# A gate's arithmetic behind the copies of all its banks, and kept-weight casts tied to the products

## The chip, the cores and the metric

The kernel runs on one core of one Trainium2 chip. The metric is device time: the microseconds (us) from start to end of one execution. The engines are named as in the profile: PE is TensorE (PEld its weight loads), DVE is VectorE, ACT is ScalarE, POOL is GpSimd, SP is SyncE, which here only issues DMAs.

## The reference, cut to what matters

One step of a hybrid decoder layer: eight heads of stick-breaking attention and four heads of gated linear attention (GLA) read one common input projection; each head's output is gated and goes through one output projection, with a norm and a residual behind it.

```python
u = h @ w_in                                   # h: rms_norm(x); sq, sk, sv, sg | gq, gk, gv, gg, ga
o_sb  = sb_prompt(q, k, v, sb_bias)            # 8 heads, 1040 positions (16 meta + 1024)
o_gla = rms_norm(gla_prompt(gq, gk, gv, gf), gla_norm_g)
mixed = concatenate([o_sb * silu(sg), o_gla * silu(gg)])
x = x + rms_norm(mixed @ w_out, norm_post_g)   # w_out: 2048 x 2048
```

The same is done for 8 sampled sequences of 4 tokens with a paged key and value cache. The change touches two pieces: `o * silu(g)` for the gates `sg` and `gg`, and the weights of the last product of `mixed @ w_out`.

## The kernel before, in words

*Input projection and gates.* `inproj` (L336) computes 128 columns of `w_in` for all tokens: 16 blocks of depth, three matmuls for each (high and low halves of both factors), the tokens in three chunks, each in a PSUM bank of its own (`acc_..._0` to `_2`; the pool has three such banks). Weights come in four chunks `wr`, are cast to `wh` on ScalarE (L187), and their rest `wl` is made on VectorE (L190). A chunk of weights thus serves four blocks of depth. When a bank is complete, `evac` is called. For a gate, `gate_group` (L528), it copies the bank to a stage `gx` on ScalarE (L532), after which the bank is free for the next group, and hands `gate_rest` (L507) to the weaver. That loads the head's output `go` from the DRAM tensor `od` (L513), and makes silu as a clamp (L516, VectorE), Exp and Ln (L517, L518, ScalarE), a maximum (L519, VectorE), Exp (L520, ScalarE), two products (L521 with `gx`, L522 with `go`, VectorE), and stores the result to `md` (L523). There are 16 gates, so 48 such pieces. `gx`, `go` and `gs` take buffers of one pool, `stg`, that has seven; a gate takes nine.

*The weaver.* `W.spawn(gen, d)` puts a piece of work on a heap; `W.beat()`, called after each two blocks of depth of a chunk, runs what is due. A gate's rest is spawned with a delay of 1, so it is written at the beat right behind its own bank's copy. The queues' order is then set by the framework's scheduler from the order of writing, from priorities (`urgent()` raises weight casts and bank copies) and from dependences; a NOSYNC dependence (`tc.add_manual_dep`) only says that one instruction stands behind another and puts no wait into the program. Each engine runs its own queue in order.

*Around gates 0 to 2.* Gate 0 runs beside the tail of the last attention head (`z`, `X`, `Y`, `hi_s`, `lo_s`, L596 to L663). VectorE meanwhile works through L470, the products of sampled queries with cached keys (`z_feed`). `od<-ost` (L687) stores the last head's output; `wal` (L861) is a cast that waits for it, for the tile that it writes lies in memory that the store reads from. After gate 2 comes the group `acc_gk` of the GLA keys.

*Output projection.* Seven products of halves (a Strassen-like scheme) for each half `q` of the columns: `step(p, q)` takes eight weight blocks `wr` from a ring of four (cast L1480 on ScalarE, rest L1481 on VectorE), and accumulates into four banks `b`, twelve matmuls for each block (L1682 to L1684). Products 7 and 4 share banks: after product 7 `take` reads them (L1547, `y`), then product 4 adds to the same banks, after which `take` reads them again (L1551, `u`). Sixteen small matmuls `sc` (L1702) for the sampled tokens end a product 7. The very last product, 4 of the second half, takes its weights from `kept`, loaded ahead by `load_keep` (L1713): eight loads `keep`, eight casts (L1723, ScalarE), eight subtractions (L1724, VectorE). `spread(ins)` (L480) puts an instruction behind `W.mark`, the newest product matmul, order only.

Of the kernel before, what the change touches and what calls it, by code (L numbers as in the profile page):

```python
# [10 lines left out]
F32 = mybir.dt.float32  # L11
# [4 lines left out]
AF = mybir.ActivationFunctionType  # L16
# [38 lines left out]
NOSYNC = mybir.DependencyInfo(mybir.DependencyClass.NoSync, mybir.DependencyReason.DATA)  # L55
# [34 lines left out]
def hybrid_step(ctx: ExitStack, tc: tile.TileContext, x_prompt, x_sample, cache_k, cache_v, state_gla,  # L90
# [5 lines left out]
    vec, act, pool = nc.vector, nc.scalar, nc.gpsimd  # L96
# [17 lines left out]
    W = Weaver()  # L114

    def stage(nm, dt=F32):
        return stg.tile([P, 384], dt, tag="stg", name=nm)
# [77 lines left out]
    with tc.tile_pool(name="xp", bufs=2) as xp, tc.tile_pool(name="xps", bufs=5, space=PSUM) as xps:  # L195
# [109 lines left out]
        for c, (lo, hi) in enumerate(XCHUNKS):  # L305
            n = hi - lo
            for k in range(NK):
# [10 lines left out]
                ins = act.activation(hh[k][:, lo:hi], ps[:, :n], AF.Copy, scale=gpre[:, k:k + 1]).ins  # L318
# [11 lines left out]
            for k in range(NK):  # L330
                wh, wl = wchunks[k]
# [4 lines left out]
    def inproj(c0, evac, lo0, nm, chunks=CHUNKS):  # L336

        acc = [accp.tile([P, 512], F32, tag="acc", name=f"acc_{nm}_{c}") for c in range(3)]
        for kk in range(NK // 2):
            if kk % 2 == 0:  # L340
                ws = weight_chunk(w_in[0], kk // 2, c0, f"{nm}_{kk // 2}")
            for c, (lo, hi) in enumerate(chunks):
                lo = max(lo, lo0)
                n = hi - lo
                for k in (2 * kk, 2 * kk + 1):
                    wh, wl = ws[k % 4]
                    mm(acc[c][:, :n], wh, hh[k][:, lo:hi], start=(k == 0), stop=False)  # L347
                    mm(acc[c][:, :n], wh, hl[k][:, lo:hi], start=False, stop=False)  # L348
                    W.mark = mm(acc[c][:, :n], wl, hh[k][:, lo:hi], start=False, stop=(k == NK - 1)).ins  # L349
                if kk == NK // 2 - 1:  # L350
                    with urgent():
                        evac(c, acc[c][:, :n], lo, hi)
                W.beat()
# [126 lines left out]
    def spread(ins):  # L480

        if W.mark is not None:
            tc.add_manual_dep(ins.ins, W.mark.name, NOSYNC, reason="spread")
# [24 lines left out]
    def gate_rest(g, lo, hi, x):  # L508
        n = hi - lo
        e = min(hi, REAL) - lo  # L510
        o = stage(f"go{g}_{lo}")
        w = n if g >= 8 else e
        nc.sync.dma_start(o[:, :w], od[g][:, lo - META:lo - META + w])  # L513
        st = stage(f"gs{g}_{lo}")
        s, x = st[:, :n], x[:, :n]
        vec.tensor_scalar(s, x, -1.0, 30.0, ALU.mult, ALU.min)  # L516
        act.activation(s, s, AF.Exp)  # L517
        act.activation(s, s, AF.Ln, bias=1.0)  # L518
        vec.scalar_tensor_tensor(s, x, -1.0, s, ALU.mult, ALU.max)  # L519
        act.activation(s, s, AF.Exp, scale=-1.0)  # L520
        vec.tensor_tensor(s, s, x, ALU.mult)  # L521
        vec.tensor_tensor(s[:, :w], s[:, :w], o[:, :w], ALU.mult)  # L522
        nc.sync.dma_start(md[g][:, lo - META:hi - META], s)  # L523
        return
        yield

    evacs = []

    def gate_group(g):
        def evac(c, ps, lo, hi):  # L530
            x = stage(f"gx{g}_{c}")
            evacs.append(act.copy(x[:, :hi - lo], ps).ins)  # L532
            W.spawn(gate_rest(g, lo, hi, x), 1)
        inproj(C_SG + g * P if g < 8 else C_GG + (g - 8) * P, evac, META, f"g{g}")


# [260 lines left out]
    with tc.tile_pool(name="gp", bufs=1) as gp, tc.tile_pool(name="gps", bufs=1, space=PSUM) as gps:  # L797
# [20 lines left out]
        def slot(c):  # L818

            return 8 if c == 8 else 4 * (1 - c % 2) + c // 2  # L820
# [540 lines left out]
    with ExitStack() as out:  # L1361
# [99 lines left out]
        def behind_ring(ins):  # L1461
            tc.add_manual_dep(ins, newest[0].name, NOSYNC, reason="behind")
# [251 lines left out]
        def load_keep():  # L1714

            keep.extend(slot(REGION["B"][i], f"keep{i}") for i in range(4))
            kept.extend([keep[k // 2][:, (2 * (k % 2) + i) * 512:(2 * (k % 2) + i + 1) * 512] for i in range(2)] for k in range(8))
            for k in range(12):
                if k < 8:
                    behind_ring(nc.sync.dma_start(kept[k][1].bitcast(F32), td[3][:, k, 512:1024]).ins)  # L1720
                if k > 3:
                    wh, wl = kept[k - 4]
                    act.copy(wh, wl.bitcast(F32))  # L1723
                    vec.tensor_tensor(wl, wl.bitcast(F32), wh.bitcast(F32), ALU.subtract)  # L1724
                yield 2

        kept = []
        AFTER = {(1, 1): lambda: W.spawn(form(5, 2)), (2, 1): lambda: W.spawn(form(3, 2), 8), (6, 1): lambda: W.spawn(form(7, 2)),
                 (5, 1): lambda: W.spawn(form(4, 1)),
                 (3, 1): lambda: (W.spawn(finish0()), W.spawn(load_keep(), 1))}  # L1730
        for pair in ((1, 2), (6,), (5, 3), (7, 4)):
            for q in range(2):
# [48 lines left out]
```

## Time and profile before

| | us |
|---|---|
| median of three runs | 2034.35 (2033.86 to 2036.96) |
| the profiled execution's own time | 2034.71 |
| its span, first to last instruction | 2033.0 |
| PE busy | 2004.2 (99%) |
| DVE busy | 1496.9 (74%) |
| ACT busy | 1018.4 (50%) |

Engine times are sums over the span. A matmul's duration in the trace is longer than the distance to the next one's start, since matmuls overlap; what a matmul costs is read from the distance of starts. A bracket behind an instruction gives the idle time of its engine ahead of it and what ended that time.

### The profile page before, as it was taken

The page shows a single profiled execution, that of the slowest core. Times are in us where ns is not written, and L with a number is a line of the kernel's source. Part 1 is how long each engine was busy: PE and PEld are TensorE (multiplying, and loading weights), DVE is VectorE, ACT ScalarE, POOL GpSimd, SP SyncE. Part 2 cuts the span into 40 slices and gives each one's busy share as a digit, 9 for nine tenths or more (in the row PEclk, how much of TensorE's full clock was granted, in tenths as well). Part 3 has the DMA queues.
Part 4 walks back from the last instruction along what each step waited for, and adds up shares of the span by engine and source line. Part 5 has one row for each costly group of instructions (what it writes and reads, how often), then busy time and mean ns, then how long its engine had stood idle before and what let it go on. Part 6 is the DMA issues. An engine that isn't in the chain of part 4 may idle for free.

```text
span 2033.0 us, 41746 instructions
## 1 busy us (share of the span) xinstructions
PE 2004.2 (99%) x12379; PEld 1852.4 (91%) x12379; DVE 1496.9 (74%) x6163; ACT 1018.4 (50%) x2377; POOL 96.1 (5%) x355
## 2 busy tenths in 40 slices
PE   6999999999999999999999999999999999999998
PEld 5999999999999999999999999999988898788776
DVE  7368888888888888899898888978444338365466
ACT  7356767675766757433535335254433335343342
POOL 0111110101000010000000000000000000000000
PEclk9999999999999999999999999999999999999999
DMA  6345554545555442433342434335767656352485
GB/s 205 98 136 161 143 163 132 175 129 157 151 161 151 141 125 77 142 101 89 103 108 80 126 79 120 90 93 176 243 220 234 221 186 221 104 176 94 141 281 204
DMA packets 371980, 301.92 MB, mean 149 GB/s; under 512 B 42336, under 2 KB 312264, under 8 KB 371752
## 3 DMA queue, kind: packets, MB, share of 16 engines
q1 hardware_dynamic: 371448, 298.73, 49.1%
q8 instruction: 97, 1.59, 0.3%
q14 instruction: 131, 1.07, 0.2%
q10 hardware_dynamic: 304, 0.53, 0.1%
HBM read 241.84 MB, written 57.31 MB: 147 GB/s over the span
## 4 chain that ended last, share of the span: by engine, by line
PE 91%; DVE 3%; DMA 2%; ACT 2%; issue 1%; SPq 0%; DVEq 0%; POOL 0%; POOLq 0%; ACTq 0%
PE acc_g L347 6%; PE acc_g L348 5%; PE acc_g L349 5%; PE b L1682 4%; PE b L1683 4%; PE b L1684 4%; PE acc_gv L347 3%; PE acc_gv L348 3%; PE acc_gv L349 3%; PE acc_k L347 3%; PE acc_k L349 3%; PE acc_k L348 3%; PE acc_q L348 3%; PE acc_q L347 3%; PE acc_q L349 3%; PE acc_v L347 3%
## 5 line engine op out<-in xcount | busy, mean ns | idle before, releaser
L470 DVE SCALAR_TENSOR_TENSOR jk<-kp,qb 128x128 f32<-128x128 f32 x2048 | 593.6, 290 | 46.2 <-DMA qb<-qsd 3.0
L347 PE MATMUL acc_g<-hT,wh_g 128*128 128x368 f32 (+2 forms) x768 | 250.7, 326 | 0.0
L348 PE MATMUL acc_g<-hT,wh_g 128*128 128x368 f32 (+2 forms) x768 | 247.2, 322 | 0.0
L349 PE MATMUL acc_g<-hT,wl_g 128*128 128x368 f32 (+2 forms) x768 | 246.9, 321 | 0.0
L470 DVE DVE_READ_ACCUMULATOR jk<-kp,qb 128x1 f32 x2048 | 167.3, 82 | 0.0
L1682 PE MATMUL b<-ring,f 128*128 128x512 f32 x416 | 163.9, 394 | 1.5 <-DVE y L1547 1.1
L1683 PE MATMUL b<-ring,f 128*128 128x512 f32 x416 | 162.3, 390 | 0.0
L1684 PE MATMUL b<-ring,f 128*128 128x512 f32 x416 | 161.9, 389 | 0.0
L347 PEld LDWEIGHTS acc_g<-hT,wh_g 128*128 128x128 f32 x768 | 144.3, 188 | 12.0 <-issue 10.7
L348 PEld LDWEIGHTS acc_g<-hT,wh_g 128*128 128x128 f32 x768 | 144.4, 188 | 0.7
L349 PEld LDWEIGHTS acc_g<-hT,wl_g 128*128 128x128 f32 x768 | 144.2, 188 | 0.0
L1481 DVE TENSOR_TENSOR ring<-wr,ring 128x512 fp32r<-128x512 f32 x104 | 71.2, 689 | 97.7 <-ACT ring L1480 97.1
L1480 ACT CAST ring<-wr 128x512 fp32r<-128x512 f32 x104 | 64.0, 620 | 134.7 <-PE b L1684 78.1
L347 PE MATMUL acc_gv<-hT,wh_gv 128*128 128x402 f32 (+2 forms) x384 | 130.1, 339 | 0.0
L347 PE MATMUL acc_k<-hT,wh_k 128*128 128x384 f32 (+1 forms) x384 | 126.1, 328 | 0.0
L348 PE MATMUL acc_gv<-hT,wh_gv 128*128 128x402 f32 (+2 forms) x384 | 125.3, 326 | 0.0
L349 PE MATMUL acc_gv<-hT,wl_gv 128*128 128x402 f32 (+2 forms) x384 | 125.0, 326 | 0.0
L349 PE MATMUL acc_k<-hT,wl_k 128*128 128x384 f32 (+1 forms) x384 | 124.7, 325 | 0.0
L348 PE MATMUL acc_k<-hT,wh_k 128*128 128x384 f32 (+1 forms) x384 | 124.4, 324 | 0.0
L347 PE MATMUL acc_q<-hT,wh_q 128*128 128x368 f32 (+2 forms) x384 | 124.3, 324 | 0.0
L348 PE MATMUL acc_q<-hT,wh_q 128*128 128x368 f32 (+2 forms) x384 | 123.6, 322 | 0.0
L349 PE MATMUL acc_q<-hT,wl_q 128*128 128x368 f32 (+2 forms) x384 | 123.3, 321 | 0.0
(483 smaller groups left out, 5263.6 us busy)
## 6 DMA issues: line engine op xcount, KB each, us to landing
kp<-in_cache_k_dram SPq DMA_DIRECT2D x512, 64.0 KB
vr<-in_cache_v_dram SPq DMA_DIRECT2D x64, 512.0 KB
qb<-qsd SPq DMA_DIRECT2D x64, 256.0 KB
wr_g<-in_w_in_dram SPq DMA_DIRECT2D x64, 256.0 KB
wr<-td SPq DMA_DIRECT2D x56, 256.0 KB
tf<-in_w_out_dram SPq DMA_DIRECT2D x48, 256.0 KB
td<-tf SPq DMA_DIRECT2D x48, 256.0 KB
wr<-in_w_out_dram SPq DMA_DIRECT2D x48, 256.0 KB
```

Of the source, the lines that this page charges most:

```text
L347: mm(acc[c][:, :n], wh, hh[k][:, lo:hi], start=(k == 0), stop=False)
L348: mm(acc[c][:, :n], wh, hl[k][:, lo:hi], start=False, stop=False)
L349: W.mark = mm(acc[c][:, :n], wl, hh[k][:, lo:hi], start=False, stop=(k == NK - 1)).ins
L470: ins = vec.scalar_tensor_tensor(jk[:], kp[:], 1.0, qbs[h, b][:, t, :], ALU.mult, ALU.mult, accum_out=zt[:, t, NPG - 1 - i:NPG - i])
L1480: act.copy(wh, r)
L1481: vec.tensor_tensor(wl, r, wh.bitcast(F32), ALU.subtract)
L1682: mm(bk[:], ah, wh, start=first and k == 0, stop=False, skip_group_check=True)
L1683: mm(bk[:], ah, wl, start=False, stop=False, skip_group_check=True)
L1684: W.mark = mm(bk[:], al, wh, start=False, stop=last and k == 7, skip_group_check=True).ins
```

## The change

Two edits. In `gate_rest` the first Exp stands, by an order-only dependence, behind the newest bank copy, and the rest of bank `c` is spawned with a delay of 3 − c beats instead of 1: all three rests of a gate are now written at the same beat, behind the copy of the third bank. In `load_keep` the cast of a kept weight is put behind the newest product matmul. One line is added, so lines of the new kernel beyond 517 count one more.

```diff
--- before.py
+++ after.py
@@ -514,7 +514,8 @@
         st = stage(f"gs{g}_{lo}")
         s, x = st[:, :n], x[:, :n]
         vec.tensor_scalar(s, x, -1.0, 30.0, ALU.mult, ALU.min)
-        act.activation(s, s, AF.Exp)
+        ins = act.activation(s, s, AF.Exp)
+        tc.add_manual_dep(ins.ins, evacs[-1].name, NOSYNC, reason="behind")
         act.activation(s, s, AF.Ln, bias=1.0)
         vec.scalar_tensor_tensor(s, x, -1.0, s, ALU.mult, ALU.max)
         act.activation(s, s, AF.Exp, scale=-1.0)
@@ -530,7 +531,7 @@
         def evac(c, ps, lo, hi):
             x = stage(f"gx{g}_{c}")
             evacs.append(act.copy(x[:, :hi - lo], ps).ins)
-            W.spawn(gate_rest(g, lo, hi, x), 1)
+            W.spawn(gate_rest(g, lo, hi, x), 3 - c)
         inproj(C_SG + g * P if g < 8 else C_GG + (g - 8) * P, evac, META, f"g{g}")
 
 
@@ -1720,7 +1721,7 @@
                     behind_ring(nc.sync.dma_start(kept[k][1].bitcast(F32), td[3][:, k, 512:1024]).ins)
                 if k > 3:
                     wh, wl = kept[k - 4]
-                    act.copy(wh, wl.bitcast(F32))
+                    spread(act.copy(wh, wl.bitcast(F32)))
                     vec.tensor_tensor(wl, wl.bitcast(F32), wh.bitcast(F32), ALU.subtract)
                 yield 2
```

The number of instructions on each engine is the same. What stands where, at three places (names are tile and buffer number; an output stands ahead of `<-`):

ScalarE after gate 2; `gx` is a bank's copy, `gs_16` and `gs_384` the first and second piece of the gate's arithmetic, `wh_gk` a weight cast of the next group. Before:

```order
L532 COPY gx_0_15356<-acc_g_0_14983 128x368
L517 ACTIVATE gs_16_15360<-gs_16_15360 128x368
L532 COPY gx_1_15375<-acc_g_1_14984 128x384
L518 ACTIVATE gs_16_15360<-gs_16_15360 128x368
L532 COPY gx_2_15415<-acc_g_2_14985 128x304
L187 CAST wh_gk_1_15569<-wr_gk_1_15567 128x512
L520 ACTIVATE gs_16_15360<-gs_16_15360 128x368
L517 ACTIVATE gs_384_15400<-gs_384_15400 128x384
```

Now:

```order
L533 COPY gx_0_15356<-acc_g_0_14983 128x368
L533 COPY gx_1_15364<-acc_g_1_14984 128x384
L187 CAST wh_gk_1_15569<-wr_gk_1_15567 128x512
L533 COPY gx_2_15393<-acc_g_2_14985 128x304
L517 ACTIVATE gs_16_15397<-gs_16_15397 128x368
L519 ACTIVATE gs_16_15397<-gs_16_15397 128x368
L517 ACTIVATE gs_384_15408<-gs_384_15408 128x384
L519 ACTIVATE gs_384_15408<-gs_384_15408 128x384
```

The copies of the three banks moved ahead of all of the gate's activations.

ScalarE after gate 1, before and now; `wal` is the cast that waits for the store of `ost`, `wh_g_2` and `wh_g_3` are gate 2's third and fourth weight chunk. Before:

```order
L517 ACTIVATE gs_768_14974<-gs_768_14974 128x304
L518 ACTIVATE gs_768_14974<-gs_768_14974 128x304
L520 ACTIVATE gs_768_14974<-gs_768_14974 128x304
L187 CAST wh_g_2_15189<-wr_g_2_15187 128x512
L861 CAST wal_15489<-walr 96x128
L187 CAST wh_g_3_15290<-wr_g_3_15288 128x512
```

Now:

```order
L521 ACTIVATE gs_16_14952<-gs_16_14952 128x368
L521 ACTIVATE gs_384_14963<-gs_384_14963 128x384
L862 CAST wal_15489<-walr 96x128
L517 ACTIVATE gs_768_14974<-gs_768_14974 128x304
L187 CAST wh_g_2_15189<-wr_g_2_15187 128x512
L519 ACTIVATE gs_768_14974<-gs_768_14974 128x304
L521 ACTIVATE gs_768_14974<-gs_768_14974 128x304
L187 CAST wh_g_3_15290<-wr_g_3_15288 128x512
```

`wal` moved from behind the cast of the third weight chunk to a place ahead of it, and the third piece's activations to both sides of that cast.

VectorE at the end of product 7, first half; `y_0_0` to `y_0_3` are the reads of the four banks, `keep` a kept weight, `c` finished rows of the output. Before:

```order
L1481 TENSOR_TENSOR ring_29084<-wr_7_31006,ring_29083 128x512
L1616 SCALAR_TENSOR_TENSOR c_0_29119<-c_0_29119,vrt_y_30857,xr_0_30869 128x512
L1481 TENSOR_TENSOR ring_29084<-wr_0_31054,ring_29083 128x512
L1724 TENSOR_TENSOR keep_30878<-keep_30878 128x512
L1616 SCALAR_TENSOR_TENSOR c_1_29120<-c_1_29120,vrt_y_30857,xr_1_30871 128x512
L1724 TENSOR_TENSOR keep_30878<-keep_30878 128x512
L1547 TENSOR_TENSOR y_0_0_30310<-b_0_30833,y_0_0_30310 128x512
L1547 TENSOR_TENSOR y_0_1_30312<-b_1_30834,y_0_1_30312 128x512
L1547 TENSOR_TENSOR y_0_2_30314<-b_2_30835,y_0_2_30314 128x512
```

Now:

```order
L1482 TENSOR_TENSOR ring_29084<-wr_7_31006,ring_29083 128x512
L1617 SCALAR_TENSOR_TENSOR c_0_29119<-c_0_29119,vrt_y_30857,xr_0_30869 128x512
L1482 TENSOR_TENSOR ring_29084<-wr_0_31054,ring_29083 128x512
L1617 SCALAR_TENSOR_TENSOR c_1_29120<-c_1_29120,vrt_y_30857,xr_1_30871 128x512
L1482 TENSOR_TENSOR ring_29084<-wr_1_31077,ring_29083 128x512
L1548 TENSOR_TENSOR y_0_0_30310<-b_0_30833,y_0_0_30310 128x512
L1548 TENSOR_TENSOR y_0_1_30312<-b_1_30834,y_0_1_30312 128x512
L1548 TENSOR_TENSOR y_0_2_30314<-b_2_30835,y_0_2_30314 128x512
```

The two subtractions of kept weights are gone from ahead of the bank reads, and the ring's cast of `wr_1`, which stood behind them, stands ahead.

On SP's queue after gate 1 the store of `ost` moved from behind two loads of the sampled queries' work (`kp`, `qb`), the third output load (`go_768`) and the first result's store (`md`) to a place right behind the weight load `wr_g_3`. Since all three copies now take their buffers of `stg` ahead of the rests, `go_768` takes the buffer that the first copy `gx_0` leaves when L521 of the first piece has read it, and `gs_768` the one that `gx_1` leaves.

## Rows read from the trace of the kernel before

**Rows 1.** The page: busy time of the engines, and the chain that ended last.

```profile
PE 2004.2 (99%) x12379; PEld 1852.4 (91%) x12379; DVE 1496.9 (74%) x6163; ACT 1018.4 (50%) x2377; POOL 96.1 (5%) x355
...
PE 91%; DVE 3%; DMA 2%; ACT 2%; issue 1%; SPq 0%; DVEq 0%; POOL 0%; POOLq 0%; ACTq 0%
```

**Rows 2.** What TensorE waited for: us in total, times, longest.

```profile
PE b L1682 <- DVE y L1547: 1.1, 1, 1.1
PE acc_gk L347 <- ACT gx L532: 1.0, 1, 1.0
...
PE b L1682 <- DVE u L1551: 0.3, 1, 0.3
...
PE z L654 <- DVE lo_s L599: 0.3, 1, 0.3
```

**Rows 3.** Timeline, TensorE after gate 2: start us, us, engine, line, operation.

```profile
855.36 0.34 PE L348 MATMUL acc_gk<-hT,wh_gk 128*128 128x402 f32 x1
855.54 0.35 PE L349 MATMUL acc_gk<-hT,wl_gk 128*128 128x402 f32 x1
856.84 0.44 PE L347 MATMUL acc_gk<-hT,wh_gk 128*128 128x386 f32 x1 [0.96 <-ACT gx L532]
```

**Rows 4.** Timeline, ScalarE after gate 2.

```profile
852.97 0.47 ACT L532 COPY gx<-acc_g 128x368 f32<-128x368 f32 x1 [3.37 <-PE acc_g L349]
855.91 0.51 ACT L517 ACTIVATE gs<-gs 128x368 f32<-128x368 f32 x1 [2.48 <-DVE gs L516]
856.33 0.46 ACT L532 COPY gx<-acc_g 128x384 f32<-128x384 f32 x1
```

**Rows 5.** Timeline, TensorE at the ends of products 7 and 4.

```profile
1951.94 1.07 PE L1702 MATMUL sc<-wr,small 128*32 128x256 f32 x16
1954.15 0.47 PE L1682 MATMUL b<-ring,f 128*128 128x512 f32 x1 [1.13 <-DVE y L1547]
...
1976.93 0.39 PE L1683 MATMUL b<-ring,f 128*128 128x512 f32 x1
1977.16 0.39 PE L1684 MATMUL b<-ring,f 128*128 128x512 f32 x1
1977.89 0.50 PE L1682 MATMUL b<-ring,f 128*128 128x512 f32 x1 [0.34 <-DVE u L1551]
...
1999.82 1.07 PE L1702 MATMUL sc<-wr,small 128*32 128x256 f32 x16
2000.82 0.50 PE L1682 MATMUL b<-keep,f 128*128 128x512 f32 x1
```

**Rows 6.** Timeline, ScalarE in the output projection.

```profile
1950.79 1.28 ACT L1723 CAST keep<-keep 128x512 fp32r<-128x512 f32 x2 [2.74 <-DMA keep<-td]
...
1974.02 0.62 ACT L1723 CAST keep<-keep 128x512 fp32r<-128x512 f32 x1 [5.29 <-DMA keep<-td]
...
1993.08 0.62 ACT L1480 CAST ring<-wr 128x512 fp32r<-128x512 f32 x1 [7.40 <-DMA wr<-td]
```

**Rows 7.** Timeline, VectorE: the four bank reads after product 7.

```profile
1953.31 2.48 DVE L1547 TENSOR_TENSOR y<-b,y 128x512 f32<-128x512 f32 x4
```

**Rows 8.** Timeline after gate 1: SP's store, and ScalarE's cast that waits for it.

```profile
834.93 0.70 SPq L687 DMA_DIRECT2D od<-ost x1
...
841.91 0.30 ACT L861 CAST wal<-walr 96x128 fp32r<-96x128 f32 x1 [3.75 <-DMA od<-ost]
```

**Rows 9.** Timeline, gate 2: first matmul of chunks three and four, and VectorE's `wl`.

```profile
843.20 0.33 PE L347 MATMUL acc_g<-hT,wh_g 128*128 128x368 f32 x1
...
847.89 0.68 DVE L190 TENSOR_TENSOR wl_g<-wr_g,wh_g 128x512 fp32r<-128x512 f32 x1
...
848.92 0.33 PE L347 MATMUL acc_g<-hT,wh_g 128*128 128x368 f32 x1
```

**Rows 10.** Windows: busy us of PE, PEld, DVE, ACT, POOL; clock, DMA share, GB/s.

```profile
1955.00:1965.00 10.00, 10.00 (x46) 8.25 (x45) 9.81 (x18) 5.48 (x14) 0.00 (x0) 1.00 0.87 295
1965.00:1975.00 10.00, 10.00 (x46) 8.29 (x45) 3.63 (x6) 2.25 (x5) 0.00 (x0) 1.00 0.90 303
```

## The prediction, made before the result was known

> **What bounds the kernel now.** The page's first part and its chain come first [rows 1]: TensorE is busy 2004.2 of 2033.0 us and carries 91% of the chain that ended last; its granted clock is 1.00 in the windows [rows 10], the 2.4 GHz level. So an edit on ScalarE, VectorE or a queue can be worth no more than the time for which TensorE stands still. The second view is TensorE's list of waits [rows 2]. Its start-up entries lie outside the edit; of the rest four are of a size to matter: a product of the output projection waiting for `y` (1.1 us), `acc_gk` waiting for a gate's copy `gx` (1.0), a product waiting for `u` (0.3), and an attention product waiting for `lo_s` (0.3). The third view is TensorE's own rows at three of these places, for what each costs against the pitch of starts there.
>
> After gate 2 [rows 3] the starts are 0.18 us apart, and then 855.54 is followed by 856.84: 1.30 for a step of 0.18, so 1.12 us lost. In the output projection [rows 5] the sixteen small `sc` matmuls that begin at 1951.94 are followed by the next product at 1954.15, 2.21 later; the same sixteen at 1999.82 are followed after 1.00. Lost: 1.21 us. At 1977.16 the next start is 0.73 away where the pitch is 0.23: 0.50 us. Together 2.83 us, the most that removing these waits can return.
>
> Why they wait is read on ScalarE. After gate 2 [rows 4] it copies bank 0 at 852.97, then stands 2.48 us at L517 of the same piece, for a clamp (L516) that VectorE has not got to, and only at 856.33 copies bank 1, with no wait of its own: the copy was held by the queue alone. `acc_gk` needs that bank. In the projection [rows 6] ScalarE stands 2.74 us at a cast of kept weights (L1723) until their load lands, at 1950.79, and once more 5.29 us until 1974.02. VectorE has the matching subtractions ahead of L1547, which therefore reads the banks only from 1953.31 [rows 7]; the product that accumulates into the same banks waits for it.
>
> **The change part by part.** *Nothing is added or removed*: the same activations, copies, casts and DMAs with the same shapes; only order-only dependences and delays differ. So there is no term for work, only for waits gone and waits new.
>
> *Gate part, gone.* In the new order bank 1's copy stands right behind bank 0's and L517 behind all three. The 2.48 us wait then falls on ScalarE when no bank is held: −1.12 us after gate 2. The other fifteen gates have no such entry in TensorE's waits [rows 2], so nothing comes back there.
>
> *Gate part, new.* Each gate's arithmetic starts one to two pieces later, its three pieces nearly together. After gate 0 this falls into the attention's tail, where TensorE has its 0.3 us wait for `lo_s` [rows 2]. I walked ScalarE and VectorE through the new order with the durations of the rows of before and find `lo_s` ready within some 0.3 us of its time now; I allow −0.3 (that wait goes) to +0.5. After gate 1 the cast `wal` (L861) moves ahead of the cast of gate 2's third weight chunk, and `wal` waits for a store, `od<-ost`: issued at 834.93, and ScalarE stood 3.75 us until 841.91 for it [rows 8]. The store itself moves ahead of four transfers on SP's queue; my walk has it issued 1.3 to 2 us earlier, so that with its present 6.98 us (841.91 − 834.93) `wal` runs near 840, and the two casts behind it are through by 842. They are wanted at 843.20 [rows 9]. So no new stall is likely; price if it comes, below.
>
> The Trainium skill weighs in here: "DMA: Bandwidth & Descriptors", section "Anatomy of one DMA — SWDGE (gpsimd) path", gives a DMA about 2.0 us fixed plus its bytes at 436 GB/s. That would be an estimate of 2.6 us for this 256 KB store, against 6.98 in the row, where it shares the engines with other transfers; by the page `wal` would run near 836, the new wait could not occur, and the sum would be 2031.5 instead of my 2031.8. The measured row decides, since the page's figure is for one transfer alone.
>
> *Kept weights, gone.* The eight casts and eight subtractions move behind products, into 1957 to 1995, when their loads have long landed. L1547 then has only a ring cast ahead of it. Bank 0 of the ending product is complete four banks' work before its end (12 × 0.23 = 2.8 us), so `y` has time for bank 0 (2.48 / 4 = 0.62 us, rows 7) before the small matmuls end: −1.21 us. The same reasoning at 1977.16: −0.50 us.
>
> *Kept weights, new.* Eight subtractions, each like the 0.68 us one of the same shape in rows 9, 5.4 us of VectorE, enter a stretch that was 98% busy from 1955 to 1965 but 36% from 1965 to 1975 [rows 10]; the ring's casts there run ahead of the products, and a delay of two subtractions (1.4 us) moves into the emptier ten. The last two casts now stand behind the ring cast of 1993.08 [rows 6]: 1993.08 + 3 × 0.62 + 0.68 = 1995.6 at the latest by these durations, and the product from kept weights begins at 2000.82 [rows 5], so 5 us of cover hide them. With that cover gone each microsecond late would be a microsecond lost. I take zero; bounds 0 to +0.5.
>
> *The sum.* −1.12 − 1.21 − 0.50 = −2.83. New waits between −0.3 and +1.8 (0.5 after gate 0, 0.8 after gate 1, 0.5 in the projection); I take +0.3, nearer the lower end because each walk came out with cover. Net −2.5. The profiled execution took 2034.71 us (its span of 2033.0 and 1.7 around it): 2034.71 − 2.5 = 2032.2. The median of the three timed runs, 2034.35, is 0.36 lower, so on its scale **2031.8 us**. This is 0.12%. About 0.2% (4.1 us) is what a measurement of this kernel can tell from no change, so the forecast is "within 0.2%".
>
> **The rivals.** *The store holds the weights.* The removed wait on a bank is replaced by one on `od<-ost`. For: `wal` really moves ahead of a weight cast, and its wait was the longest ScalarE had there. If the store lands at 841.91 as now, the chain `wal` 0.30, L517 0.51, weight cast 0.62, subtraction 0.68 ends at 844.0, where TensorE wants the low half at about 843.5: +0.5; if it lands 0.3 later, +0.8; and the fourth chunk, whose low half is done at 847.89 + 0.68 = 848.57 and wanted at 848.92, a cover of 0.35 us [rows 9], may lose the same again. Up to +1.3 on top of −2.83: **2032.8**. Against: the store is issued earlier.
>
> *The waits only move.* In the new order a ring cast of `wr_1` stands ahead of L1547, where it stood behind; it waits for a load, and ring casts have waited up to 7.40 us for theirs [rows 6]. If that load lands as late as the kept one did, near 1950.8, the product stalls as before; with the bank after gate 2 given back in the next group, nothing is left: **2034.4**. Against: the row of 1951.94 was held by the kept load, issued behind `wr_1`.
>
> *Slower: weights behind a gate's loads.* The stages' seven buffers are taken in another order: the third output load of a gate (`go…_768`) now needs the buffer of `gx…_0`, so on SP's queue it waits until VectorE is through L521 of the first piece, and the next weight loads stand behind it. If VectorE, itself waiting for the gate's earlier loads, holds it by a wait like the 3.75 us of rows 8, the next chunk with its cover of 0.35 is 3.4 us late. In one group that only eats the gain (+3.4 − 2.83 = +0.6, 2034.9); if all three groups behind the attention do it, +10.2 − 2.83 = +7.4: **2041.7**. It decides from a weight load more than its cover late. Against: most chunks have several microseconds of cover, and the queue shifts by a slot or two.
>
> *Much faster.* The Trainium skill ("Perfetto Trace Analysis", section "Identifying the Most-Contended Engine") calls matmul busy time a bad measure of headroom and points to the busy time of weight loads. Weight loads are busy 91% [rows 1], which would leave some 180 us. As a mechanism: matmuls that are counted busy while they in truth wait for casts would speed up too. Against it stand the equal pitches, 0.18 and 0.23 us, wherever no wait is named [rows 3, 5]: those matmuls are paced by their columns. More than 4.1 us would take all three waits and nearly half as much again; a time of **2030**.
>
> **How the numbers follow.** Forecast (2031 to 2032.4) 0.62; the store holds the weights 0.14; the waits only move 0.10; slower 0.09; much faster 0.05. The range takes the first three with the bounds of the new waits: low 2030.6 (all waits gone, the one for `lo_s` too, and 0.6 for the runs' own spread), high 2034.8 (gain gone, and 0.4 more). That leaves out 0.14. Faster by over 0.2%: 0.05; slower: 0.09; within: 0.86.
>
> **What would show it.** Right: after gate 2 `gx_0` and `gx_1` stand back to back on ScalarE and the entry `acc_gk` <- `gx` is gone; the entries for `y` and `u` are gone, and 1.00 us lies between the `sc` matmuls and the next product; L1723's casts show no wait for a DMA. Wrong: `acc_g` waiting for `wl_g` near 843 or 849 (the store), a ring cast waiting for its load ahead of L1547 (waits move), weight loads issued late behind `go` (slower), or a product waiting for `keep` after 2000. A changed pitch of matmuls with no wait named would break the whole reading.

## The result, and the profile after

The changed kernel takes 2038.67 us (median of 14 runs, 2036.53 to 2040.35) against 2034.13 us for the kernel before (14 runs beside it): ratio 1.0020, 95% interval 1.0013 to 1.0027. It is slower by 4.5 us, 0.22%, where 2.5 us of gain was forecast. The profiled execution took 2039.21 us, its span was 2037.3, and TensorE is still busy for 98% of it.

All three waits that the prediction wanted to remove are gone. After gate 2 the two copies and the third stand without an activation between them, and TensorE goes from 855.60 to 855.78, a plain step of 0.18 us where [rows 3] had 1.30. Timeline of the changed kernel, ScalarE and TensorE (answers to [rows 3, 4]), then TensorE where products 7 and 4 of the first half meet and end ([rows 5]):

```profile
853.04 0.47 ACT L533 COPY gx<-acc_g 128x368 f32<-128x368 f32 x1 [3.33 <-PE acc_g L349]
854.08 0.48 ACT L533 COPY gx<-acc_g 128x384 f32<-128x384 f32 x1 [0.57 <-PE acc_g L349]
...
856.40 0.51 ACT L517 ACTIVATE gs<-gs 128x368 f32<-128x368 f32 x1 [0.71 <-DVE gs L516]
...
855.60 0.34 PE L349 MATMUL acc_gk<-hT,wl_gk 128*128 128x402 f32 x1
855.78 0.34 PE L347 MATMUL acc_gk<-hT,wh_gk 128*128 128x386 f32 x1
...
1958.22 1.07 PE L1703 MATMUL sc<-wr,small 128*32 128x256 f32 x16
1959.22 0.50 PE L1683 MATMUL b<-ring,f 128*128 128x512 f32 x1
...
1982.29 0.39 PE L1685 MATMUL b<-ring,f 128*128 128x512 f32 x1
1982.52 0.39 PE L1683 MATMUL b<-ring,f 128*128 128x512 f32 x1
```

1.00 us now lies between the small matmuls and the next product, 0.23 ahead of the last row: no loss at either place.

TensorE's list of waits, however, has three new entries of 0.7 us or more, and that for `lo_s` has grown (answer to [rows 2]; us in total, times, longest):

```profile
PE Us L1110 <- DVE km L1107: 2.8, 1, 2.8
...
PE b L1683 <- ACT u L1530: 0.9, 1, 0.9
PE z L655 <- DVE lo_s L600: 0.9, 2, 0.6
...
PE C L1291 <- ACT cn L1264: 0.7, 1, 0.7
```

The first is at gate 3, in a part of the program that the prediction did not speak of: beside this gate a GLA head updates the states of its eight sampled sequences. For each, VectorE makes masked keys `km` (L1107), TensorE multiplies them with the values into `Us` (L1110), and VectorE adds that to the decayed old state (L1112); the new state `sn` is a stage of the pool `stg`, as are `km` and the gate's `gx`, `go` and `gs`. Timeline of SP, VectorE and TensorE there:

```profile
1378.84 0.32 SPq L524 DMA_DIRECT2D md<-gs  x1
...
1384.63 0.48 DVE L1112 SCALAR_TENSOR_TENSOR sn<-Sb,ebl,Us 128x256 f32<-128x256 f32 x1 [3.08 <-DMA md<-gs]
1385.03 0.94 DVE L522 TENSOR_TENSOR gs<-gs,gx 128x384 f32<-128x384 f32 x2
1385.88 0.90 DVE L523 TENSOR_TENSOR gs<-gs,go 128x384 f32<-128x384 f32 x2
1386.70 0.28 DVE L1107 TENSOR_SCALAR km<-pk,rmask 96x128 fp32r<-96x128 f32 x1
...
1383.91 0.30 PE L347 MATMUL acc_g<-hT,wh_g 128*128 128x304 f32 x1
1387.03 0.39 PE L1110 MATMUL Us<-pv,km 96*128 96x256 f32 x1 [2.81 <-DVE km L1107]
```

Read from the bottom: TensorE stands 2.81 us for `km`. VectorE has `km` behind four of the gate's products, and these behind a new state that stands 3.08 us until the store `md<-gs` has landed. The store is that of gate 3's own first piece, issued at 1378.84. Nothing in the arithmetic links the two: the new state was given the buffer from which the store still reads. The addresses in the built program say the same: this state, the second of the eight, has the buffer that the gate's first piece held just before, where in the kernel before it has one that an output stage `gst` of the GLA head held. There the first piece's store is issued at 1373.59, and the same state waits for nothing (kernel before):

```profile
1378.99 0.47 DVE L1111 SCALAR_TENSOR_TENSOR sn<-Sb,ebl,Us 128x256 f32<-128x256 f32 x1
```

Behind this stand-still the matmuls themselves become slower. Windows of TensorE: us, busy (x matmuls), granted clock, DMA share, GB/s:

```profile
1387.00:1388.00 1.00, 0.97 (x7) 1.00 0.83 301
1388.00:1389.00 1.00, 1.00 (x6) 0.78 0.32 111
1389.00:1390.00 1.00, 1.00 (x4) 0.50 0.40 138
...
1391.00:1392.00 1.00, 1.00 (x5) 0.51 0.69 146
1392.00:1393.00 1.00, 1.00 (x9) 1.00 0.75 242
```

For some three us the granted clock is 0.50, the 1.2 GHz level, and only four or five matmuls fall into a window, where nine do at 1.00.

**Where the time went, in one table.** For each profile I took the start of the same matmul in it and in the profile of the kernel before, as the median over 15 matmuls from a point on, and how that difference changes across five places (positive: lost there). The last column is the profiled execution's own time; the kernel before's is 2034.71. The runs are told in the next section.

| profile | gate 2 (840 to 870) | gate 3 (1370 to 1400) | product `C` (1400 to 1430) | start of the projection (1700 to 1735) | `y`, `u` (1940 to 1990) | own time |
|---|---|---|---|---|---|---|
| after | −1.22 | +4.66 | +0.99 | +1.70 | −1.82 | 2039.21 |
| after, again (e11) | −1.22 | +4.41 | +1.10 | +1.33 | −1.82 | 2038.80 |
| e1, gates only | −1.23 | +4.37 | +1.02 | +1.30 | +0.44 | 2040.52 |
| e2, casts only | −1.20 | 0.00 | 0.00 | 0.00 | −1.82 | 2031.75 |
| e3, not gate 3 | −1.23 | −0.02 | −0.01 | +1.69 | −1.82 | 2032.91 |
| e4, gate 2 and casts | −1.23 | −0.03 | −0.01 | 0.00 | −1.82 | 2031.37 |
| e5, state in place | −1.22 | +3.59 | +0.81 | +0.75 | −1.82 | 2037.86 |
| e12, the same again | −1.22 | +7.03 | +0.84 | +1.74 | −1.82 | 2041.39 |
| e6, not 3 and 15 | −1.23 | +0.01 | −0.01 | +1.92 | −1.82 | 2033.99 |
| e10, not 3, 14, 15 | −1.23 | −0.06 | 0.00 | 0.00 | −1.82 | 2031.30 |
| e9, gate 3 and casts | +0.41 | +5.22 | +0.72 | −0.01 | −1.82 | 2039.06 |
| e7, before, again | −0.18 | −0.03 | −0.01 | 0.00 | +1.60 | 2035.80 |
| e8, gate 2 only | −1.22 | −0.02 | 0.00 | 0.00 | +1.80 | 2036.62 |

For the changed kernel: −1.22 − 1.82 won, 4.66 + 0.99 + 1.70 = 7.35 lost; the balance of +4.3 is nearly all of the 4.5 us between the two profiled executions.

### The profile page after: what moved, and what is told of

The parts are those of the page before. It is cut to its first block, busy times and chain, and to the rows that moved or that the text cites. A ratio compares the mean times of both kernels' runs of the same rounds, so it can differ in the third digit from the quotient of the medians.

```text
span 2037.3 us, 41721 instructions
## 1 busy us (share of the span) xinstructions
PE 2006.2 (98%) x12379; PEld 1853.3 (91%) x12379; DVE 1497.3 (73%) x6163; ACT 1021.4 (50%) x2377; POOL 97.6 (5%) x355
## 4 chain that ended last, share of the span: by engine, by line
PE 89%; DVE 4%; DMA 3%; ACT 2%; issue 1%; SPq 0%; DVEq 0%; ACTq 0%
PE acc_g L347 5%; PE acc_g L348 5%; PE acc_g L349 5%; PE b L1683 4%; PE b L1684 4%; PE b L1685 4%; PE acc_gv L347 3%; PE acc_gv L348 3%; PE acc_gv L349 3%; PE acc_k L347 3%; PE acc_k L349 3%; PE acc_k L348 3%; PE acc_q L348 3%; PE acc_q L347 3%; PE acc_q L349 3%; PE acc_v L347 3%
```

## The experiments

Theory A: the loss sits at gate 3, where the new state takes a buffer that is being stored, with its echoes further on; the rest of the change does what was predicted. The rivals are named in each expectation. Times stand beside those of the kernel before on the same chip, and ratios are against these. In a built program the order-only dependence alone moves no instruction, and the delays alone move every one that the gate part moves; so "the gate part" below is the delays. It can be had gate by gate:

```diff
-        tc.add_manual_dep(ins.ins, evacs[-1].name, NOSYNC, reason="behind")
+        if g in GATES:
+            tc.add_manual_dep(ins.ins, evacs[-1].name, NOSYNC, reason="behind")
...
-            W.spawn(gate_rest(g, lo, hi, x), 3 - c)
+            W.spawn(gate_rest(g, lo, hi, x), 3 - c if g in GATES else 1)
```

**e1, the gate part alone** (all gates; against the changed kernel):

```diff
-                    spread(act.copy(wh, wl.bitcast(F32)))
+                    act.copy(wh, wl.bitcast(F32))
```

> The gate part alone; the kept weights' casts as before. Theory A (the gate part lost 7.3 us in new waits, the keep part gave 1.7): slower than the full change by the 1.7 us of the two projection waits, about 2034.1 + 4.5 + 1.7 = 2040.3; the wait of Us for km near 1384 is there (2.8 us), the waits for y and u of before are back. Theory B (the moved kept-weight casts cost the time, somewhere in the projection): about 2033, for only the 1.1 us after gate 2 is gained.

Measured: 2042.18 us (5 runs), ratio 1.0038 (1.0024 to 1.0052). All three new losses are in the table, and the loss at `y` is back. It is 1.9 us above the 2040.3 expected. 1.4 of that is the base: the kernel before took 2035.5 beside it, where the expectation started from 2034.1. The wait for `y` was 1.5 us in this profile where it had been 1.1 [rows 2].

**e2, the casts alone** (no gate in the new order):

> The keep part alone; the gates as before. Theory A: 2034.1 - 1.7 = 2032.4, no wait of Us for km, the waits of 1951.94 and 1977.16 gone, the one of acc_gk for gx still there. Theory B: slower than before, 2037 to 2039.

Measured: 2031.83 us (10 runs), ratio 0.9984 (0.9974 to 0.9993). No new loss anywhere: these belong to the gate part. Two things were not expected. The gain is larger than 1.7 us, and the wait after gate 2 is absent though the gates stand as in the kernel before; e7 below takes this up.

**e3, both parts but gate 3 as before**, and **e4, gate 2 and the casts**, which ask whether gate 3 carries the loss and whether the rest of the gates matter:

> Both parts, but the gate beside the sampled states (gate 3) keeps its old order. Theory A1 (the wait near 1384 comes from a buffer of stg that the third new state gets from this gate's first piece, whose store is still running): that wait, the low clock behind it and the late chain at 1425 go, 2038.7 - 4.5 - 1.0 = 2033.2, and TensorE keeps only the waits near 1720 (1.4 us). Theory A2 (it is the later arithmetic of gates in general that crowds VectorE): little changes, 2037 to 2039.

> Both parts, but of the gates only the one ahead of acc_gk (gate 2) gets the new order. Theory A: all three waits of before gone and none of the new ones come: 2034.1 - 2.8 = 2031.3, the fastest so far. If the order after gate 2 alone already turns the buffers of stg for what follows (rival), the wait of Us near 1384 comes back in some size: 2033 to 2037.

Measured: e3 2032.87 us (10 runs), ratio 0.9988 (0.9979 to 0.9998); e4 2031.70 us (10 runs), ratio 0.9983 (0.9974 to 0.9993). Leaving gate 3 in its old order takes away 5.8 us of 2038.67, and with it the half clock and the wait at `C`: in the table both columns are zero. `C`, a product for the sampled tokens, is thus an echo: it waits for ScalarE's copy `cn` (L1264), which empties the one bank that `C` can take, and the work ahead of that copy runs over the engines that gate 3 held up. The store `zd<-zt` near its start is issued at 1415.62 in the profile after and at 1409.77 in the one before, 5.9 us later, where TensorE itself is 3.5 us later. What e3 still has over e4 is the loss at the start of the projection.

**e5, the new state in place.** If it is the buffer, then it must help to give that state no new buffer:

```diff
-                sn = stage(f"sn{g}_{b}")[:, :DV]
+                sn = Sb if (g, b) == (3, 1) else stage(f"sn{g}_{b}")[:, :DV]
```

> The changed kernel, but at gate 3 the second new state is written over the old one instead of into a new buffer of the shared pool (nothing is left out). Theory A (the new state takes the buffer of gate 3's first piece and waits for its store, and TensorE's half clock follows from that stand-still): VectorE's 3.08 us wait, TensorE's 2.81 us wait for km, the stretch at a granted clock of 0.50 and the 0.69 us wait at C all go, the waits beside units 8 and 9 of the last stage stay; 2038.7 - 2.8 - 1.6 - 0.9 = 2033.3 us, as when gate 3 is left old. Rival B (VectorE has simply more of the gate's arithmetic queued before km, whatever the buffer): km stays late, 2037 or more. Rival C (the wait moves on to the third km, whose buffer is then another piece's that is still being stored): a wait of 1 to 3 us at the next Us, 2035 to 2038.

Measured: 2040.41 us (10 runs), ratio 1.0019 (1.0010 to 1.0028), as slow as the changed kernel. The state no longer waits, but the next taker of the buffer does, and that is the third `km` itself. Timeline of SP, VectorE and TensorE of this kernel:

```profile
1380.09 0.37 SPq L524 DMA_DIRECT2D md<-gs  x1
...
1379.00 0.47 DVE L1112 SCALAR_TENSOR_TENSOR Sb<-Sb,ebl,Us 128x256 f32<-128x256 f32 x1
1385.96 0.28 DVE L1107 TENSOR_SCALAR km<-pk,rmask 96x128 fp32r<-96x128 f32 x1 [2.98 <-DMA md<-gs]
...
1386.30 0.38 PE L1110 MATMUL Us<-pv,km 96*128 96x256 f32 x1 [3.10 <-DVE km L1107]
```

So A's remedy failed and rival C came true: the expectation started from 2034.1 us, and 1.0019 times that is 2038, the upper end of its 2035 to 2038. It is the stronger evidence for the buffer: the wait follows the buffer, from one instruction to another, and ends with the same store. In this built program the third `km` has the address of the gate's first piece. No run gave the pool an eighth buffer. Rival B, a VectorE that is merely too full, is out: the engine stands idle for 2.98 us ahead of `km`.

**e9, gate 3 alone in the new order**, with the casts:

> Gate 3 alone in the new order, with the spread casts; the fifteen other gates as before. Theory A (the whole loss at gate 3 is local: the second new state takes the buffer of gate 3's first piece): VectorE's wait of some 3 us at that state, TensorE's 2.8 us wait for km and the wait at C come back, and the time is that of gate 2 alone with the casts, 2031.7, plus 4.4 to 5.5: 2036.1 to 2037.2 us. Rival (the loss needs the other gates' shifts too): no wait at gate 3, 2031 to 2032.5 us.

Measured: 2038.78 us (10 runs), ratio 1.0014 (1.0004 to 1.0023), against 2031.70 for the same with gate 2 in place of gate 3. The whole loss at gate 3 is local to it. VectorE and TensorE there, and the windows behind:

```profile
1386.81 0.48 DVE L1113 SCALAR_TENSOR_TENSOR sn<-Sb,ebl,Us 128x256 f32<-128x256 f32 x1 [3.65 <-DMA md<-gs]
...
1389.21 0.58 PE L1111 MATMUL Us<-pv,km 96*128 96x256 f32 x1 [3.38 <-DVE km L1108]
```

```profile
1390.00:1391.00 1.00, 1.00 (x6) 0.50 0.52 188
...
1393.00:1394.00 1.00, 1.00 (x8) 1.00 0.44 71
```

It came out 1.6 us above the expected range: the store let the state wait 3.65 us instead of 3.08, and the wait after gate 2, whose order is the old one here, was 1.4 us.

**e6 and e10: the start of the projection.** VectorE and ScalarE of the changed kernel there:

```profile
1725.94 0.69 DVE L1386 TENSOR_TENSOR s<-s,s 128x512 f32<-128x512 f32 x1 [2.80 <-DMA s<-md]
...
1726.67 0.62 ACT L1413 CAST f<-s 128x512 fp32r<-128x512 f32 x1 [3.08 <-DVE s L1386]
```

The sum `s` is late because its load from `md` is, and ScalarE stands 3.08 us for it; behind that cast in its queue are the copies `u` (L1530), for which TensorE waits. I took gate 15, the last one, for the cause, then gate 14 too:

> Both parts, but gates 3 and 15 as in the kernel before. Theory D (gate 15's late store delays the state s in the last stage, so the cast of f, and behind it on ScalarE the copies of u): the 0.89 us wait for u goes too, and the time is that with gate 3 alone left old, 2032.9, less 0.7 to 1.2: 2032.0 us, that of the kernel with gate 2 alone changed. Rival: the wait comes from the spread casts of the kept weights and stays: 2032.9.

> Both parts, but gates 3, 14 and 15 as before. Theory G (gate 14's later arithmetic pushes gate 15's, its last store and with it SP's weight loads and the state s in the last stage): no wait for u, gate 15's last store before 1706 us instead of 1709.84, and a time 0.7 to 1.2 below that with gates 3 and 15 old: 2031.6 to 2032.1 us. Rival (the delay builds up over all the gates): u still waits 0.5 us or more, 2032.8 us.

Measured: e6 2032.80 us (10 runs), ratio 0.9983 (0.9974 to 0.9993); e10 2031.38 us (10 runs), ratio 0.9980 (0.9970 to 0.9989). Theory D fell: with gate 15 in its old order the loss stays (+1.92 in the table). Theory G held: with gate 14 old too, it is zero. SP's queue in e6, and below it in e10; the last `md<-gs` is gate 15's third piece:

```profile
1709.84 0.32 SPq L525 DMA_DIRECT2D md<-gs  x1
...
1710.93 1.81 SPq L1481 DMA_DIRECT2D wr<-in_w_out_dram  x4
1713.57 0.42 SPq L1371 DMA_DIRECT2D s<-md  x1
```

```profile
1704.47 0.32 SPq L525 DMA_DIRECT2D md<-gs  x1
...
1706.36 2.08 SPq L1481 DMA_DIRECT2D wr<-in_w_out_dram  x4
1709.18 1.43 SPq L1371 DMA_DIRECT2D s<-md  x1
```

With gate 14's later arithmetic gate 15's last store goes out 5.4 us later, though gate 15 is written as before; 0.6 of that is e6 as a whole, whose TensorE is that much later here already. In SP's in-order queue the first projection weights stand behind that store and come 4.6 us later, and the load of `s` 4.4. In between the lateness grows step by step: gate 14's last store goes out at 1686.61 instead of 1684.38, gate 15's first clamp (L516) starts at 1697.39 instead of 1694.69 and its third at 1703.83 instead of 1700.52, among sums of `s` (L1387) on VectorE, one of which waits 0.87 us for its load from `md`. Whether gate 14 alone would do it, with the gates ahead of it in the old order, no run asks.

**e7, the kernel before profiled again**, and **e8, gate 2 alone without the casts**, on what the two predicted gains are worth:

> The kernel before, profiled a second time. If the 0.96 us wait after gate 2 hangs on how long the store od<-ost took in the one execution (6.98 us there; 5.93 us in the run of the keep part alone, where the gates stand as before and the wait was absent), then it is anything from 0 to 1 us here and goes with that store. Rival: it belongs to the order of the instructions and is 0.96 again.

> Only gate 2's arithmetic behind its three copies, the casts as before. The prediction's term: 2034.1 - 1.1 = 2033.0 us. If the wait after gate 2 is present only in some executions of the kernel before, less: 2033.3 to 2034.1; the trace shows no wait after gate 2 and y and u waits of 1.16 and 0.4 us in the projection as before.

Measured: e7 one execution, 2035.80 us; e8 2034.71 us (11 runs), ratio 0.9990 (0.9981 to 0.9999), above the 2033.0 to 2034.1 expected, but with the kernel before at 2036.22 beside it. With gate 2 in its old order there are now four profiles. ScalarE's cast `wal`, which ends the store's wait ([rows 8] for the kernel before), and TensorE's start after gate 2 ([rows 3]) in e2, e7 and e9:

```profile
840.61 0.30 ACT L861 CAST wal<-walr 96x128 fp32r<-96x128 f32 x1 [2.54 <-DMA od<-ost]
...
855.64 0.35 PE L347 MATMUL acc_gk<-hT,wh_gk 128*128 128x386 f32 x1
```

```profile
841.48 0.30 ACT L861 CAST wal<-walr 96x128 fp32r<-96x128 f32 x1 [3.57 <-DMA od<-ost]
...
856.39 0.44 PE L347 MATMUL acc_gk<-hT,wh_gk 128*128 128x386 f32 x1 [0.76 <-ACT gx L532]
```

```profile
842.30 0.30 ACT L863 CAST wal<-walr 96x128 fp32r<-96x128 f32 x1 [4.13 <-DMA od<-ost]
...
857.24 0.45 PE L347 MATMUL acc_gk<-hT,wh_gk 128*128 128x386 f32 x1 [1.35 <-ACT gx L534]
```

With the cast at 840.61, 841.48, 841.91 (the kernel before) and 842.30 the wait is 0, 0.76, 0.96 and 1.35 us. The chain between: VectorE's subtraction for `wal` stands for that cast and its whole queue with it, the clamp L516 among it, for which ScalarE stands with bank 1's copy behind. So the later that one store lands, the longer the wait after gate 2. (`wal` does not lie in `ost` itself: in the built program it has memory of an earlier tile of the attention's pool, and its wait counts this store all the same.)

Gate 2's new order may only move this lateness on. In e8 the cast ran as late as 842.38 and no wait is left after gate 2, but `acc_gq`, the next group, waits for VectorE's `wl_gq` at 879.98 and 897.94 (0.47 and 0.22 us), and the starts from 870 to 900 lose 1.3 us, which is in no column of the table. In e2 and e4 they lose 0.3 and 0.4 us there, in the kernels with gate 1 in the new order at most 0.05. That the late store is behind these losses too is argued, not shown.

The wait for `y` varies in the same way; ahead of it stands the cast of a kept weight, which waits for its load [rows 6]: 1.13 [rows 5], 1.5 in e1, and in e8 and e7:

```profile
1952.02 1.07 PE L1704 MATMUL sc<-wr,small 128*32 128x256 f32 x16
1954.95 0.47 PE L1684 MATMUL b<-ring,f 128*128 128x512 f32 x1 [1.85 <-DVE y L1549]
```

```profile
1954.87 0.47 PE L1682 MATMUL b<-ring,f 128*128 128x512 f32 x1 [2.25 <-DVE y L1547]
```

**e11 and e12, second profiles** of the changed kernel and of e5, on the half clock:

> The changed kernel, profiled a second time. The waits at km, C and u come again, with 2.5 to 3.1, 0.5 to 0.8 and 0.5 to 0.9 us. The half clock behind the wait at km: if it belongs to a stand-still of this length, there is a stretch of some 3 us at 0.50 again; if it hangs on something that differs from execution to execution (with the state in place TensorE stood 3.1 us and the clock stayed at 1.00), it may be absent, and the excess over the kernel before is 1.6 us less at that place.

> The kernel with the second new state of gate 3 written in place, profiled a second time. TensorE stands about 3 us for km again. If the half clock behind such a stand-still is a matter of the single execution, this one may show it (a stretch of about 3 us at 0.50 between 1386 and 1392); if it belongs to the program, to what TensorE runs around the stand-still, the clock stays at 1.00 here too, as in this kernel's first profile.

Measured: e11 2038.80 us, e12 2041.39 us, one execution each. e11 shows the three waits again (2.5, 0.8 and 0.6 us) and again three us at 0.50. e12 stood 4.11 us and its clock fell, where e5, the same program, stood 3.10 us at 1.00. Windows of e5, then of e12:

```profile
1387.00:1388.00 1.00, 1.00 (x11) 1.00 0.30 83
1389.00:1390.00 1.00, 1.00 (x8) 1.00 0.54 202
```

```profile
1387.00:1388.00 1.00, 1.00 (x7) 0.50 0.44 138
1389.00:1390.00 1.00, 1.00 (x5) 0.50 0.71 257
```

So the half clock doesn't belong to the order of the instructions alone; what decides it in an execution stays open.

**The better version.** e4 (2031.70 us) and e10 (2031.38 us) both beat the kernel before, by ratios of 0.9983 and 0.9980 whose intervals end at 0.9993 and 0.9989. From each other, and from e2 with the casts alone (2031.83 us), they can't be told.

## Why the prediction was wrong, point by point

*The bound and the three waits: right.* TensorE bounds the kernel, and each of the three places gives back what its rows promised: −1.22 for −1.12 at gate 2, −1.82 for −1.21 − 0.50 in the projection. (The table compares with the very execution from which the rows were read; other executions of the kernel before give other sizes, below.) With only these, as in e4 and e10, the profiled executions take 2031.37 and 2031.30 us, 0.5 below the 2034.71 − 2.83 = 2031.9 that the sum gives before its new waits.

*"The other fifteen gates have no such entry in TensorE's waits [rows 2], so nothing comes back there": the step that failed.* True of gains, and used as if it were true of losses. The change moves the arithmetic of all sixteen gates, and I walked the engines through it after gates 0 and 1 only. At gate 3 other takers of the same seven buffers stand beside the gate, and they were met by the store of a piece that is now later: +4.66, with +0.99 as its echo at `C`. Before the projection gate 14's lateness runs on through SP's queue: +1.70. The new waits were taken as +0.3 with a bound of +1.8; they were +7.35. The price of a new place couldn't be read from the rows used, but that there were sixteen places was plain from the diff, and that the states use `stg` from the code.

*New waits after gates 0 and 1: right.* The place of the first was misread, though. The 0.3 us entry for `lo_s` in [rows 2] is in the middle of the attention, and the longer one of the list after stands ahead of every gate, whose first bank copy is at 799; so neither has to do with the edit. The kernel before, then the changed one:

```profile
462.52 0.50 PE L654 MATMUL z<-lo_s,ntri 128*128 128x512 f32 x1 [0.27 <-DVE lo_s L599]
```

```profile
130.28 0.40 PE L655 MATMUL z<-lo_s,ntri 128*128 128x284 f32 x1 [0.61 <-DVE lo_s L600]
```

In gate 0's tail, from 800 to 820, TensorE gains 0.26 us in each of the eight profiles with gate 0 in the new order. That this is the size allowed for a wait that goes (0.3) is luck. `wal` did move up without holding the weights:

```profile
836.93 0.30 ACT L862 CAST wal<-walr 96x128 fp32r<-96x128 f32 x1 [1.12 <-DMA od<-ost]
```

The store was issued at 833.00. I had the cast near 840, because I kept the old 6.98 us for the store; it took 3.9, and 3.8 to 4.2 in all eight profiles with gate 1 in the new order. The Trainium skill's page ("DMA: Bandwidth & Descriptors", section "Anatomy of one DMA — SWDGE (gpsimd) path") had given an estimate of 836, nearer here. But that section is on transfers that GpSimd issues, and this store is issued by SP; no row here shows its 2.6 us either, and in the old place the same store took 5.9 to 7.4.

*Kept weights, new: right.* The bounds were 0 to +0.5, and no product waits for `keep`.

*The sizes as read from one execution: only a sample.* Both gains stand in waits that a DMA ends, and their size changes from execution to execution: 0 to 1.35 us at gate 2, and in the projection between nothing and 1.8 us more than in the profile I read. So the casts are worth more than the −1.71 of the sum (e2: 0.9984 of 2035.5, 3.3 us, with an interval from 1.4 to 5.3), and what gate 2 adds to them in the median the runs don't resolve (e4 against e2). By itself it gained 0.1% (e8).

*The rivals.* "Slower: weights behind a gate's loads" had the right resource, the seven buffers taken in another order, and not far off a time (2041.7). It looked for the victim in SP's weight loads in the groups behind the attention, and its "against" was about their cover. The victim was a buffer's next user on VectorE, with TensorE behind it in the GLA part. "The store holds the weights" and "the waits only move" did not occur in the changed kernel; e8, with gate 2 alone, shows the second in part. "Much faster" neither: where no wait and no half clock stands, the pitches are 0.18 and 0.23 us as before.

## What to carry to other kernels

Where pieces of work take buffers from a shared pool, moving one of them in time changes who gets which buffer; so look at every user of the pool at every place that the edit reaches, and ask whose store is still reading. Make such an edit where the trace shows the wait, and leave the other places as they are: the casts alone, gate 2 with the casts, or all but gates 3, 14 and 15 gain 0.2%, while the edit on all sixteen gates loses 0.2%. And a wait that a DMA ends has no fixed price in one profile; a second profile of the same kernel is a cheap way to see how it spreads.

## What the runs showed of the hardware

The granted clock fell to 0.50 around a short stand-still of TensorE: of the six profiles in which it stood 2.5 to 4.1 us for `km`, five show it, for some 3 us and in e12 for over 6, and one (e5, 3.10 us) does not. Stand-stills of 0.96 [rows 3], 1.13 [rows 5], 1.85 (e8) and 2.25 us (e7) left it at 1.00. Its price can be estimated from the table: the loss at gate 3 less the wait itself is 1.85 us in the profile after (4.66 − 2.81), 1.9 in e11 (4.41 − 2.5) and 1.84 in e9 (5.22 − 3.38), but 0.49 in e5 (3.59 − 3.10). So the clock cost some 1.4 us, half as much again as the wait in the profile after; in e12, where it was low for over 6 us, the excess is 2.92 us (7.03 − 4.11).

A store from a buffer does not always take the same time. The chain of waits of the profile after gives gate 3's first piece, from issue to landing:

```profile
1378.84 5.76 DMA md<-gs
```

The 256 KB of `od<-ost` took 3.8 to 7.4 us in the fourteen profiles, read as the time from its issue to `wal`. A buffer is taken for that long after its last arithmetic.
